# The lag-kernel matmuls of a state space layer, given by steps over four column positions

## The chip, the cores and the metric

The kernel runs on one core of a Trainium2 chip. The metric is the device time of one execution in microseconds (us), lower is better. TensorE is called PE here, VectorE DVE, ScalarE ACT, GpSimd POOL, and SyncE, whose queue starts most transfers, SP.

## The reference, cut to what matters

Two layers of a hybrid backbone over 512 latent tokens and 256 context tokens of 1024 channels. Each layer has three mixers (spatial gating, a bidirectional diagonal state space, pooling), an output projection and a SwiGLU feed-forward. The change touches the state space alone, of which the reference computes, for each of 32 groups of 16 channels with 64 states and in two directions:

```python
def diag_scan(lam_bar, bu, h0, reverse):
    ...
    _, h = lax.associative_scan(combine, (a, bu), reverse=reverse, axis=1)
    return h

    for k, reverse in enumerate((False, True)):
        lam_bar, b_bar = ssm_discretize(lam_re[k], lam_im[k], log_dt[k], b_re[k], b_im[k])
        cm = lax.complex(c_re[k].astype(jnp.float32), c_im[k].astype(jnp.float32))
        ...
        h_lat = diag_scan(lam_bar, bu_lat, h_end, reverse)
        y_lat = y_lat + jnp.einsum('ghp,blgp->blgh', cm, h_lat).real
```

The kernel computes this in chunks of 8 tokens. Inside a chunk, what a token gives to one at a distance of m tokens is a 16 x 16 matrix per group, the real part of C lam^m B, for m from -7 to 7. These matrices are the lag kernels.

## The kernel before, in words

Products of float32 with float32 are made from split operands (`mm3`, lines 144 to 146: three matmuls of a high and a low part). The small ones of the state space's tables are float32 matmuls by `mm` (line 149), each of which appears in the trace as two records. The accumulators in PSUM are tiles named acc, aux, pr and md; pr and md have one buffer each.

`ssm_prep` makes a layer's tables, block by block. In layer 0 a block has 8 groups (4 blocks, before the mixers, while the input projection runs); the powers X, XF and Y of B and C lie in one buffer named pz. In layer 1 a block has 4 groups (8 blocks, made beside the feed-forward of layer 0); X, XF and Y have tiles of their own names. bb holds B, Cc holds C. A block goes through: the turn tables (Tt), the powers X by DVE and ACT, a reversed copy XF, their transposes on PE (line 599) for the table E, the powers Y (line 543 in layer 0), and the lag kernels.

The lag kernels (lines 627 to 646) are made in two halves, each into a tile pr. A matmul handles two groups: its weights are 32 columns of bb, and its output lies on 32 partitions of pr, the column position j (0 to 3 in layer 0, 0 and 1 in layer 1; the `tile_position` 0, 32j). For each j and each of the real and imaginary parts i, the first half has one matmul with Cc (128 rows by 32 columns of the array, 32 columns of data) and one with Y (64 rows by 32 columns, 224 columns of data). The second half has one matmul for each j and i, with XF (64 rows by 32 columns, 224 columns of data, at row 64). ACT (line 648) and DVE (line 649) then take the result into klag, and POOL's queue stores it as Kd, from where the mixer loads it as T.

The kernel is written for a framework whose scheduler sets each engine's order from its own estimate of the times. Where a change alters those, the order of other work near it moves as well. The fillers of layer 1's tables and the modulation vectors (tiles wm from w_mod, bm and md) are issued between the steps of the feed-forward and of the mixers.

Of the kernel before, what the change touches and what calls it, by code (L numbers as in the profile page):

```python
# [86 lines left out]
def tile_backbone(ctx, tc, A, out):  # L87
# [65 lines left out]

    # ------------------------------------------------------------- constants
    ident = cst.tile([128, 128], F32, name="ident")
# [34 lines left out]

    # ------------------------------------------------------------ modulation
    def first_mod_loads():
        """w_mod for the first shift and scale, by blocks of 256 channels: [block][shift, scale][chunk]."""
        big_ = bigt([128, 3, 8, 256], F32, "wmod")
        where = {(0, 0): "rawm", (0, 1): "raw", (1, 0): "whi", (1, 1): "wlo", (2, 0): 0, (2, 1): 1, (3, 0): 2,
                 (3, 1): "rawm"}
        res = {}
        for (j, m), w in where.items():
            c_ = slice(1024 * m + 256 * j, 1024 * m + 256 * j + 256)
            if isinstance(w, int):  # L200
                t = big_[:, w]
                dma(t, A["w_mod"][0, :, c_].rearrange("(t p) c -> p t c", p=128))
                res[j, m] = [t[:, k] for k in range(8)]
            else:
                res[j, m] = []
                for h in range(2):
                    t = wp.tile([128, 4, 256], F32, tag=w, name=nm("wm"), bufs=2)
                    dma(t, A["w_mod"][0, 512 * h:512 * h + 512, c_].rearrange("(t p) c -> p t c", p=128))
                    res[j, m] += [t[:, k] for k in range(4)]
        return res  # L210
# [48 lines left out]
    def mod_rows_v(l, m, res, lanes):  # L259
        """The same rows with the products summed over the chunks on the vector engine."""  # L260
        accs = [q4([128, 1024], s="macc") for _ in range(lanes)]
        for k in range(8):
            raw = wp.tile([128, 1024], F32, name=nm("wm"), tag="rawm", bufs=2)
            dma(raw, A["w_mod"][l, k * 128:(k + 1) * 128, m * 1024:(m + 1) * 1024])
            for r in range(lanes):
                c_ = csil[:, 2 * k + r:2 * k + r + 1]
                if k == 0:
                    V.tensor_scalar(accs[r], raw, c_, None, op0=ALU.mult)
                else:
                    V.scalar_tensor_tensor(accs[r], raw, c_, accs[r], op0=ALU.mult, op1=ALU.add)  # L270
            yield
        bm = wp.tile([1, 1024], F32, name=nm("bm"), tag="rawm", bufs=2)
        dma(bm, A["b_mod"][l:l + 1, m * 1024:(m + 1) * 1024])
        ps = mdt()
        for j in range(4):
            c_ = slice(256 * j, 256 * j + 256)
            mm(ps[32 * j:32 * j + 32, :256], bc(ident[0:1, 0:1], [1, 32]), bm[:, c_], start=True, stop=False,
               tile_position=(0, 32 * j))
        for r in range(lanes):
            for j in range(4):  # L280
                mm(ps[32 * j:32 * j + 32, :256], osel[:, 31 - r:63 - r], accs[r][:, 256 * j:256 * j + 256],
                   start=False, stop=r == lanes - 1, tile_position=(0, 32 * j))
        M = sp.tile([128, 256], F32, tag="M", name=nm("M"), bufs=1)
        S.copy(M, ps[:, :256])
        res.append(M)
# [44 lines left out]

    # ------------------------------------------------------------ norm -> hT
    def sumsq(x, junk):
# [4 lines left out]
    def norm_tile(x, dg, junk):  # L337
        """The RMS factors of a tile's tokens, as a diagonal that the transpose multiplies by."""
        ss = sumsq(x, junk)
        r = rsq(ss, 1, 1.0 / D)  # L340
        S.activation(dg, ident, AF.Copy, scale=r[:, 0:1])
# [32 lines left out]

    # ------------------------------------------------------------ SSM tables
    ssm = {}

    def ssm_params():
# [10 lines left out]
        def expo(x, t, h, sc):  # L389
            # exp(x) - 1 = sc * h + (sc - 1), sc a power of two; x is overwritten, h becomes sc * h  # L390
            V.tensor_scalar(t, x, 1.0 / math.log(2.0), MAGIC_EXP, op0=ALU.mult, op1=ALU.add)
# [56 lines left out]
        V.tensor_mul(qi, t, inv)  # L448
        # transposed, [(k,p), quantity, l, g]: lam, turn, q with pairs (-im, im), and the decay
        PT = cst.tile([128, 8, 2, G], F32, name="PT")  # L450
# [34 lines left out]
    def cmul(o, a_, b_, t):  # L485
        """o = a * b for pairs (re, im) [128, 2, groups, n]; b per group, (re, (-im, im))."""
        shape = list(o.shape)
# [11 lines left out]
    def prep_load(l):  # L499
        """B and C of a layer: B with (k, state) on the partitions, C with (group, channel)."""  # L500
        Br, Cr = q4([128, 2, 512], s="Br"), q4([128, 2, 4, 2, 64], s="Cr")
# [7 lines left out]
    def ssm_prep(l, Br, Cr, bufs=None):  # L509
        """The layer's tables for the chunks, block by block of 8 groups; the two directions lie on  # L510
        the partitions, (direction, state); C and its powers are kept conjugated."""
        lam, lamc = ssm["lam"], ssm["lamc"]
# [22 lines left out]
        def last_step(T, p):  # L535
            """T[4:8] = T[0:4] * p for every group, the products by the real part on the scalar engine."""
            for g in range(ng):
# [18 lines left out]
        for g0 in range(0, G, ng):  # L556
# [71 lines left out]
            for half in range(2):  # L628
                ps = prt()
                n = (128, 112)[half]  # L630
                pv = ps[:, :2 * n].rearrange("p (g c) -> p g c", g=2)
                for j in range(ng // 2):
                    jr = slice(32 * j, 32 * j + 32)
                    g2 = slice(2 * j, 2 * j + 2)
                    for i in range(2):
                        c0 = 16 * g0 + 32 * j
                        lh = bb[:, i, c0:c0 + 32]
                        if half == 0:
                            mm(pv[jr, :, 0:16], lh, Cb[:, i, g2, :], start=i == 0, stop=False,
                               tile_position=(0, 32 * j))  # L640
                            mm(pv[jr, :, 16:128], lh[0:64],
                               Y[0:64, i, g2, 0:7, :].rearrange("p g m h -> p g (m h)"),
                               start=False, stop=i == 1, tile_position=(0, 32 * j))
                        else:
                            mm(pv[jr], lh[64:128], XF[64:128, i, g2, 1:8, :].rearrange("p g m h -> p g (m h)"),
                               start=i == 0, stop=i == 1, tile_position=(64, 32 * j))
                o = slice(112, 240) if half == 0 else slice(0, 112)
# [8 lines left out]

    # ------------------------------------------------------------ the mixers
    def load_small(l):
# [53 lines left out]
    def mix_C_lat(l, pz, i, pbd, mac, poolL):  # L712
        """Tiles i and i + 1, whose z share a bank."""
        q = f4([128, 1024], "cmix")
# [29 lines left out]
    def ssm_UV(l, bt, U, vt, ET=None):  # L744
        """The chunks' inputs to the states, the backward direction's in its own order."""
        Et, tab = ET or load_ET(l, bt, q4([128, 1024], s="E"), q4([128, 768], s="tab"))
# [22 lines left out]
    def ssm_rot(l, bt, vt, tab, wk):  # L769
        """The states at the chunks' starts: turn, scan, turn back."""  # L770
        T1, T2, T3, S_, dec = wk
# [26 lines left out]
    def ssm_y(l, bt, U, FT, S_, yst, g_):  # L798
        """The outputs of a block's groups, moved to (group, channel) on the partitions, tokens (t, c)."""
        Ft, T_ = FT  # L800
# [26 lines left out]
    def mixing(l, hhi, hlo, small, filler):  # L827
# [133 lines left out]
        next(op)  # L961
        # gate of the SSM output
        mb = bigt([128, 2, 4, 768], F32R, "mb")
# [30 lines left out]
    def square(src, ss, h):  # L994
        """The sum of squares of a column half, into its column of ss."""
        jk = f4([128, 512], "jk")
        S.activation(jk, src, AF.Square, accum_out=ss[:, h:h + 1])  # L997

    def residual(xt, u, ss):
        """xt += rms factor * u, u being the products of G and m, ss the sums of m's squares."""  # L1000
        r = rsq(ss[:, 0:1], 1, 1.0 / D, more=ss[:, 1:2])
        V.scalar_tensor_tensor(xt, u, r[:, 0:1], xt, op0=ALU.mult, op1=ALU.add)
# [5 lines left out]
    def out_proj(l, mac, Gs):  # L1008
        """A first step with the products that need only the A and C parts, then the rest."""
        lat_only = l == DEPTH - 1  # L1010
# [181 lines left out]

    # =============================================================== program
    xall = bigt([128, 6, 1024], F32, "xall")
# [136 lines left out]
```

## Time and profile before

| | us |
|---|---|
| median of 3 runs | 1600.65 (1595.11 to 1605.75) |
| span of the profiled execution | 1596.2 |
| PE busy | 1524.7 |
| DVE busy | 858.9 |
| ACT busy | 631.9 |
| POOL busy | 143.4 |

The profile is of one execution. Times in the rows are us from the start of its span. PE is TensorE's matmuls and PEld its weight loads; a busy time of PE includes the modelled end of a matmul, so records overlap and start times tell more than durations. PEclk is the granted clock of TensorE, 1.00 at full speed (2.4 GHz).

### The profile page before, as it was taken

What the parts mean: (1) busy time and instruction counts of PE and PEld (TensorE: products, weight loads), DVE (VectorE), ACT (ScalarE), POOL (GpSimd) and SP (SyncE); (2) the same over time, 40 slices, a digit from 0 to 9 for tenths busy, and PEclk for the clock granted to TensorE, in tenths of its full rate; (3) what the DMA queues carried; (4) which work ended last, traced back from release to release, by engine and by line L of the source; (5) the groups of instructions that cost most, each with busy time, mean ns of one, the idle gap of its engine ahead of it and who ended that gap; (6) DMA issues with size and microseconds to landing.
All of it is one profiled execution on the core that took longest, in us unless ns stands there. A gap on an engine that the chain in (4) does not pass through costs nothing.

```text
span 1596.2 us, 22394 instructions
## 1 busy us (share of the span) xinstructions
PE 1524.7 (96%) x8649; PEld 1243.1 (78%) x8649; DVE 858.9 (54%) x1549; ACT 631.9 (40%) x1184; POOL 143.4 (9%) x244
## 2 busy tenths in 40 slices
PE   4999999998999999999999999899898999999996
PEld 2576787787888877888878888798777888888885
DVE  7476797446464675545564334768566332333335
ACT  3466755536332233333221223655456223222222
POOL 2111220003000000000000000322002000000001
PEclk9999999999999999999999999999999999999998
DMA  9468798675133455234466322657565333332332
GB/s 290 171 188 284 254 289 276 199 221 179 53 116 99 137 181 172 91 104 122 157 201 219 93 73 85 213 169 231 149 205 191 100 106 93 94 105 93 94 104 79
DMA packets 227435, 250.71 MB, mean 157 GB/s; under 512 B 50040, under 2 KB 172132, under 8 KB 226816
## 3 DMA queue, kind: packets, MB, share of 16 engines
q1 hardware_dynamic: 217364, 214.26, 43.3%
q0 software_dynamic: 9088, 34.58, 6.1%
q8 instruction: 68, 1.11, 0.3%
q10 hardware_dynamic: 876, 0.44, 0.1%
q14 instruction: 39, 0.32, 0.1%
HBM read 206.80 MB, written 42.43 MB: 156 GB/s over the span
## 4 chain that ended last, share of the span: by engine, by line
PE 83%; DMA 7%; ACT 3%; DVE 3%; POOL 2%; SPq 1%; issue 1%; DVEq 0%; POOLq 0%; ACTq 0%
PE acc L144 20%; PE acc L146 19%; PE acc L145 19%; PE pr L149 5%; PE aux L144 4%; PE aux L146 4%; PE aux L145 4%; PE md L149 4%; PE aux L149 2%; DMA wm<-in_w_mod_dram 2%; ACT w L133 1%; DMA yd<-zslot 1%; DVE w L134 1%; POOL rs L187 1%; DMA tab<-Td 1%
## 5 line engine op out<-in xcount | busy, mean ns | idle before, releaser
L144 PE MATMUL acc<-h,w 128*128 128x512 f32 (+1 forms) x1248 | 431.1, 348 | 5.1 <-DVE h L370 2.8
L145 PE MATMUL acc<-h,w 128*128 128x512 f32 (+1 forms) x1248 | 432.1, 347 | 3.2 <-DVE h L371 3.1
L146 PE MATMUL acc<-h,w 128*128 128x512 f32 (+1 forms) x1248 | 430.3, 346 | 1.4 <-DVE w L134 1.4
L134 DVE TENSOR_TENSOR w<-raw,w 128x1024 fp32r<-128x1024 f32 x190 | 232.3, 1223 | 340.5 <-ACT w L133 327.8
L133 ACT CAST w<-raw 128x1024 fp32r<-128x1024 f32 x190 | 199.3, 1049 | 407.2 <-PE acc L145 228.9
L144 PEld LDWEIGHTS acc<-h,w 128*128 128x128 f32 x1248 | 236.9, 191 | 37.8 <-DVE h L370 3.4
L145 PEld LDWEIGHTS acc<-h,w 128*128 128x128 f32 x1248 | 237.9, 191 | 34.3 <-DVE h L371 4.3
L146 PEld LDWEIGHTS acc<-h,w 128*128 128x128 f32 x1248 | 237.8, 191 | 32.1 <-issue 2.2
L1113 DVE TENSOR_TENSOR fsg<-fsg,acc 128x512 f32<-128x512 f32 (+1 forms) x68 | 39.8, 585 | 158.7 <-PE acc L146 157.3
L145 PE MATMUL aux<-w,act 128*128 128x512 f32 x220 | 86.3, 392 | 0.0
L146 PE MATMUL aux<-w,act 128*128 128x512 f32 x220 | 86.2, 392 | 0.0
L145 PE MATMUL acc<-w,act 128*128 128x512 f32 x220 | 86.0, 391 | 0.0
L146 PE MATMUL acc<-w,act 128*128 128x512 f32 x220 | 86.0, 391 | 0.0
L144 PE MATMUL acc<-w,act 128*128 128x512 f32 x220 | 83.1, 392 | 0.0
L144 PE MATMUL aux<-w,act 128*128 128x512 f32 x220 | 83.0, 391 | 0.0
L270 DVE SCALAR_TENSOR_TENSOR macc<-wm,csil,macc 128x1024 f32<-128x1024 f32 x56 | 70.6, 1277 | 5.7 <-DMA wm<-in_w_mod_dram 5.6
L1114 ACT CAST act<-fsg 128x512 fp32r<-128x512 f32 (+1 forms) x68 | 36.5, 537 | 91.3 <-DVE fsg L1113 91.3
L1112 ACT ACTIVATE fsg<-acc 128x512 f32<-128x512 f32 (+1 forms) x68 | 34.8, 511 | 83.5 <-PE acc L146 83.5
L145 PE MATMUL acc<-w,h 128*128 128x512 f32 (+1 forms) x160 | 55.6, 348 | 0.8 <-DVE w L134 0.8
L146 PE MATMUL acc<-w,h 128*128 128x512 f32 (+1 forms) x160 | 55.4, 346 | 0.0
L185 POOL TENSOR_TENSOR rs<-ss 128x1 f32<-128x1 f32 x20 | 7.6, 381 | 526.2 <-ACT jk L997 525.3
L144 PE MATMUL acc<-w,h 128*128 128x512 f32 (+1 forms) x160 | 54.6, 353 | 0.0
(364 smaller groups left out, 2395.1 us busy)
## 6 DMA issues: line engine op xcount, KB each, us to landing
wm<-in_w_mod_dram SPq DMA_DIRECT2D x90, 512.0 KB
raw<-in_ffn_w_gate_dram SPq DMA_DIRECT2D x44, 512.0 KB
raw<-in_ffn_w_up_dram SPq DMA_DIRECT2D x44, 512.0 KB
raw<-in_ffn_w_down_dram SPq DMA_DIRECT2D x44, 512.0 KB
raw<-in_w_in_dram SPq DMA_DIRECT2D x28, 512.0 KB
raw<-in_w_out_dram SPq DMA_DIRECT2D x26, 512.0 KB
xt<-xd SPq DMA_DIRECT2D x18, 512.0 KB
Ed<-Et POOLq DMA_DIRECT2D x16, 512.0 KB, 4.6
```

The lines of the kernel that those rows point to most:

```text
L133: S.copy(hi, raw)
L134: last_v[0] = V.tensor_sub(lo, raw, hi)
L144: PE.matmul(ps, lhi, rhi, start=start, stop=False, skip_group_check=True)
L145: PE.matmul(ps, lhi, rlo, start=False, stop=False, skip_group_check=True)
L146: return PE.matmul(ps, llo, rhi, start=False, stop=stop, skip_group_check=True)
L149: return PE.matmul(ps, lhsT, rhs, start=start, stop=stop, skip_group_check=True, **k)
L185: GP.tensor_tensor(t[:, :n], ss, more, op=ALU.add)
L187: GP.tensor_scalar(t[:, :n], ss, scale, EPS, op0=ALU.mult, op1=ALU.add)
L270: V.scalar_tensor_tensor(accs[r], raw, c_, accs[r], op0=ALU.mult, op1=ALU.add)
L1112: S.activation(sg[:, :n], p1[:, :n], AF.Silu)
L1113: V.tensor_mul(sg[:, :n], sg[:, :n], p2[:, :n])
L1114: S.copy(act[0][:, fl, o:o + n], sg[:, :n])
```

## The change

The loops over position and part in the first and second half are replaced by a list of jobs, each with the number of its step, which is sorted by that number. The matmuls and their operands stay the same. In the first half the steps are Cc real, Y real, Cc imaginary, Y imaginary, each over all positions; in the second half XF real, XF imaginary. Comments and docstrings are removed as well, which changes line numbers by up to 2.

```diff
-                for j in range(ng // 2):
-                    jr = slice(32 * j, 32 * j + 32)
-                    g2 = slice(2 * j, 2 * j + 2)
-                    for i in range(2):
+                jobs = []
+                for i in range(2):
+                    for j in range(ng // 2):
                         c0 = 16 * g0 + 32 * j
-                        lh = bb[:, i, c0:c0 + 32]
+                        lh, jr, g2 = bb[:, i, c0:c0 + 32], slice(32 * j, 32 * j + 32), slice(2 * j, 2 * j + 2)
                         if half == 0:
-                            mm(pv[jr, :, 0:16], lh, Cb[:, i, g2, :], start=i == 0, stop=False,
-                               tile_position=(0, 32 * j))
-                            mm(pv[jr, :, 16:128], lh[0:64],
-                               Y[0:64, i, g2, 0:7, :].rearrange("p g m h -> p g (m h)"),
-                               start=False, stop=i == 1, tile_position=(0, 32 * j))
+                            jobs.append((2 * i, pv[jr, :, 0:16], lh, Cb[:, i, g2, :], i == 0, False, (0, 32 * j)))
+                            jobs.append((2 * i + 1, pv[jr, :, 16:128], lh[0:64],
+                                         Y[0:64, i, g2, 0:7, :].rearrange("p g m h -> p g (m h)"),
+                                         False, i == 1, (0, 32 * j)))
                         else:
...
+                jobs.sort(key=lambda job: job[0])
+                for _, o_, l_, r_, st, en, tp in jobs:
+                    mm(o_, l_, r_, start=st, stop=en, tile_position=tp)
```

The order on PE in layer 1, third block, first half, as the difference of the change against before (the operand Cc or Y names the step, the last numbers are the output's shape, x2 is two matmuls in a row):

```order
-L149 MATMUL pr_5225<-Y_5155,bb_4031 32x2x112
-L149 MATMUL pr_5225<-Cc_4032,bb_4031 32x2x16
-L149 MATMUL pr_5225<-Y_5155,bb_4031 32x2x112
-L149 MATMUL pr_5225<-Cc_4032,bb_4031 32x2x16
-L149 MATMUL pr_5225<-Y_5155,bb_4031 32x2x112
-L149 MATMUL pr_5225<-Cc_4032,bb_4031 32x2x16
-L149 MATMUL pr_5225<-Y_5155,bb_4031 32x2x112
+L149 MATMUL pr_5225<-Y_5155,bb_4031 32x2x112 x2
+L149 MATMUL pr_5225<-Cc_4032,bb_4031 32x2x16 x2
+L149 MATMUL pr_5225<-Y_5155,bb_4031 32x2x112 x2
```

The same seven matmuls, now six with one of them moved ahead, stand in the same place; the first step, Cc of both positions (before: of the first), stands some rows ahead. The other blocks of layer 1 read alike.

The order on PE in layer 0, first block, first half, of the change (pz is the buffer of Y; acc is the input projection, md the modulation, from the bias bm and the weights wm):

```order
L144 MATMUL acc_937<-h_470,w_907 128x512
L149 MATMUL pr_713<-pz_344,bb_346 32x2x112
L145 MATMUL acc_937<-h_471,w_907 128x512
L146 MATMUL acc_937<-h_470,w_908 128x512
L149 MATMUL md_973<-bm_974,ident 32x256
L149 MATMUL pr_713<-pz_344,bb_346 32x2x112
L149 MATMUL md_973<-bm_974,ident 32x256 x3
L149 MATMUL pr_713<-pz_344,bb_346 32x2x112
L149 MATMUL md_973<-wm_980,csil 32x256
L149 MATMUL pr_713<-pz_344,bb_346 32x2x112
L149 MATMUL pr_713<-Cc_347,bb_346 32x2x16 x4
L149 MATMUL pr_713<-pz_344,bb_346 32x2x112 x4
```

Before, pz and Cc alternate here without a break, eight and seven times, and bm and wm follow as x4 each. Now the first Y step lies in four pieces between them; the Cc step before it stands far ahead. In the second and third block the first Y step lies in three pieces (of 1, 2 and 1 matmuls).

The order on PE in layer 0, fourth block, first half, first of before (up to the first interruption by acc):

```order
L149 MATMUL aux_1692<-zslot_904 128x96 x4
L149 MATMUL pr_1651<-pz_344,bb_346 32x2x112
L149 MATMUL pr_1651<-Cc_347,bb_346 32x2x16
L149 MATMUL pr_1651<-pz_344,bb_346 32x2x112
L149 MATMUL pr_1651<-Cc_347,bb_346 32x2x16
L149 MATMUL pr_1651<-pz_344,bb_346 32x2x112
L149 MATMUL pr_1651<-Cc_347,bb_346 32x2x16
L144 MATMUL acc_1974<-w_1979,h_470 128x512
```

and of the change:

```order
L149 MATMUL aux_1692<-zslot_904 128x96 x4
L149 MATMUL pr_1651<-pz_344,bb_346 32x2x112 x4
L149 MATMUL pr_1651<-Cc_347,bb_346 32x2x16 x4
L149 MATMUL pr_1651<-pz_344,bb_346 32x2x112 x4
L144 MATMUL acc_1974<-w_2003,h_470 128x512
```

Here all steps are whole, and the projection's matmuls that stood between them now stand ahead. SP's order has the same transfers; between about the start of layer 0's tables and the end of its mixers, loads of w_mod, w_in, E, F and T have changed places with each other. From layer 1's mixers on, the orders of all engines are equal.

## Rows read from the trace of the kernel before

**Rows 1.** The page's head.

```profile
span 1596.2 us, 22394 instructions
```

**Rows 2.** Stretches: start:end, length, busy us (instructions) by engine, clock, DMA share, GB/s.

```profile
85.00:200.00 115.00, 115.00 (x750) 78.17 (x749) 81.66 (x243) 78.06 (x173) 21.65 (x37) 0.96 0.75 239
...
98.10:104.80 6.70, 6.70 (x37) 4.29 (x37) 5.28 (x20) 4.19 (x11) 0.00 (x0) 0.55 0.59 185
152.80:156.10 3.30, 3.30 (x10) 2.68 (x10) 1.83 (x5) 0.37 (x1) 0.00 (x0) 0.61 1.03 337
200.00:310.00 110.00, 100.15 (x815) 80.91 (x815) 73.81 (x126) 59.10 (x131) 13.51 (x13) 0.97 0.84 267
490.00:860.00 370.00, 370.00 (x2056) 293.89 (x2055) 210.83 (x348) 112.49 (x195) 22.49 (x40) 1.00 0.48 153
```

**Rows 3.** PE in time order, layer 0, block 1, first half: start, us, instruction.

```profile
92.48 0.56 PE L149 MATMUL pr<-pz,bb 64*32 64x224 f32 x2
92.97 0.25 PE L149 MATMUL pr<-Cc,bb 128*32 128x32 f32 x2
93.15 0.56 PE L149 MATMUL pr<-pz,bb 64*32 64x224 f32 x2
...
97.18 0.83 PE L149 MATMUL pr<-pz,bb 64*32 64x224 f32 x2
97.94 0.80 PE L145 MATMUL acc<-h,w 128*128 128x512 f32 x1
```

**Rows 4.** PE in time order, layer 0, block 1, second half.

```profile
104.47 0.28 PE L146 MATMUL acc<-h,w 128*128 128x256 f32 x1
104.59 0.28 PE L144 MATMUL acc<-h,w 128*128 128x256 f32 x1
104.80 0.98 PE L149 MATMUL pr<-pz,bb 64*32 64x224 f32 x16
105.71 0.38 PE L145 MATMUL acc<-h,w 128*128 128x256 f32 x1
```

**Rows 5.** The same, only what has started by 104.95 us.

```profile
104.80 0.41 PE L149 MATMUL pr<-pz,bb 64*32 64x224 f32 x4
```

**Rows 6.** PE in time order, layer 1, block 1, first half.

```profile
495.92 0.56 PE L149 MATMUL pr<-Y,bb 64*32 64x224 f32 x2
496.41 0.25 PE L149 MATMUL pr<-Cc,bb 128*32 128x32 f32 x2
496.59 0.56 PE L149 MATMUL pr<-Y,bb 64*32 64x224 f32 x2
...
498.42 0.50 PE L145 MATMUL acc<-h,w 128*128 128x512 f32 x1
```

**Rows 7.** PE in time order, layer 1, block 1, second half.

```profile
502.90 0.95 PE L149 MATMUL pr<-XF,bb 64*32 64x224 f32 x8
503.78 0.39 PE L144 MATMUL acc<-h,w 128*128 128x256 f32 x1
```

**Rows 8.** The chain that ended last, layer 0's tables: start, us, what, records.

```profile
92.55 5.46 PE pr L149 x30
...
113.91 0.57 PE md L149 x8
...
122.95 0.42 PE md L149 x3
...
124.68 0.47 PE md L149 x4
...
147.93 4.95 PE pr L149 x28
```

**Rows 9.** ACT's waits, 85 to 200 us: total us, times, longest.

```profile
ACT klag L648 <- PE pr L149: 17.4, 6, 5.4
```

**Rows 10.** The chain that ended last, layer 0's mixers.

```profile
202.78 7.93 DMA raw<-in_w_out_dram
...
212.03 6.31 DMA E<-Ed
```

More of the change, by code (lines that the diff above doesn't have):

```diff
@@ L631, in ssm_prep @@
                 pv = ps[:, :2 * n].rearrange("p (g c) -> p g c", g=2)
-                for j in range(ng // 2):
-                    jr = slice(32 * j, 32 * j + 32)
-                    g2 = slice(2 * j, 2 * j + 2)
-                    for i in range(2):
+                jobs = []
+                for i in range(2):
+                    for j in range(ng // 2):
                         c0 = 16 * g0 + 32 * j
-                        lh = bb[:, i, c0:c0 + 32]
+                        lh, jr, g2 = bb[:, i, c0:c0 + 32], slice(32 * j, 32 * j + 32), slice(2 * j, 2 * j + 2)
                         if half == 0:
-                            mm(pv[jr, :, 0:16], lh, Cb[:, i, g2, :], start=i == 0, stop=False,
-                               tile_position=(0, 32 * j))
-                            mm(pv[jr, :, 16:128], lh[0:64],
-                               Y[0:64, i, g2, 0:7, :].rearrange("p g m h -> p g (m h)"),
-                               start=False, stop=i == 1, tile_position=(0, 32 * j))
-                        else:
-                            mm(pv[jr], lh[64:128], XF[64:128, i, g2, 1:8, :].rearrange("p g m h -> p g (m h)"),
-                               start=i == 0, stop=i == 1, tile_position=(64, 32 * j))
+                            jobs.append((2 * i, pv[jr, :, 0:16], lh, Cb[:, i, g2, :], i == 0, False, (0, 32 * j)))
+                            jobs.append((2 * i + 1, pv[jr, :, 16:128], lh[0:64],
+                                         Y[0:64, i, g2, 0:7, :].rearrange("p g m h -> p g (m h)"),
+                                         False, i == 1, (0, 32 * j)))
+                        else:
+                            jobs.append((i, pv[jr], lh[64:128],
+                                         XF[64:128, i, g2, 1:8, :].rearrange("p g m h -> p g (m h)"),
+                                         i == 0, i == 1, (64, 32 * j)))
+                jobs.sort(key=lambda job: job[0])
+                for _, o_, l_, r_, st, en, tp in jobs:
+                    mm(o_, l_, r_, start=st, stop=en, tile_position=tp)
                 o = slice(112, 240) if half == 0 else slice(0, 112)
```

## The prediction

> **What bounds the kernel now.** I read the page's first part, then the windows by stretch, then TensorE's instructions in time order where the lag kernels stand, then who waits for them. The span is 1596.2 us [rows 1]; the three runs have a median of 1600.65 us, so 4.5 us (0.3%) are added to a span to compare it with runs. In the stretch in which layer 1's tables are made, 490 to 860 us, PE is busy 370.00 of 370.00 us, DVE 211 and ACT 112, and the clock is 1.00 [rows 2]: whatever PE saves there shortens the kernel, because the feed-forward matmuls stand right behind it in the same queue. In the stretch of layer 0's tables, 85 to 200 us, PE is also busy 115.00 of 115.00 us [rows 2], but DVE (82) and ACT (78) are close, and the work is chained: ACT alone stood idle 17.4 us for the lag kernels' results, once for 5.4 us [rows 9]. From 200 to 310 us PE is busy 100 of 110 us and the DMA engines 0.84 of the time [rows 2]; there the chain of work that ended last goes through loads of 6 to 8 us [rows 10].
>
> **What the lag kernels cost now.** A block has two halves. The first half multiplies on two sizes of tile: Cc, 128 rows by 32 columns, and Y (in layer 0 its name is pz, the buffer it lives in), 64 rows by 32 columns. Each float32 matmul shows as two records, so "x2" is one matmul. In layer 0 the sequence is pz, Cc, pz, Cc: starts at 92.48, 92.97, 93.15 and so on to 97.18 and the next acc at 97.94 [rows 3]. A pair takes (97.18 - 92.48) / 7 = 0.671 us, of which 0.49 from a pz to the next Cc and 0.18 from a Cc to the next pz. Layer 1 has the same steps: 495.92, 496.41, 496.59 [rows 6]. Nothing of one position runs beside another here.
>
> The second half has one size of tile only, and the code before gives it position by position too. Yet its 16 records (four positions, four records each) take 105.71 - 104.80 = 0.91 us [rows 4], four of them have started by 104.95 [rows 5], and with two positions in layer 1 the 8 records take 503.78 - 502.90 = 0.88 us [rows 7]. So four positions already run side by side there, and two more positions cost 0.03 us. I conclude two things. The second halves gain nothing from the new order. And what keeps the first half serial is the change of tile size between Cc and Y, which now comes at every matmul.
>
> The Trainium skill, "TensorE: Matmul & The Clock Gate", Part 3, section "The mechanism", speaks against this: matmuls start and end strictly in program order, and a weight load runs beside a matmul in flight only where the row group differs, and the four column positions share theirs. By that rule the second half of before would be serial, and the new order would overlap nothing (0 us gained); by rows 4, 5 and 7 it is not serial, and the measurement decides.
>
> **The change, step by step.** It adds and removes no matmul and no DMA: 4 x (16 + 8) in layer 0 and 8 x (8 + 4) in layer 1 make 192 before and after. With equal steps together, a first half has four stages: Cc, Y, Cc, Y. A stage is priced by the single matmul plus what further positions cost in the second halves (0.01 to 0.02 us each): with four positions Y 0.49 + 0.04 = 0.53 and Cc 0.18 + 0.04 = 0.22; with two, 0.505 and 0.195.
>
> Layer 1, eight blocks of two positions. Before, the first Cc stands alone earlier and then seven matmuls stand together: 498.42 - 495.92 = 2.50 us [rows 6]. After, the order has Y x2, Cc x2, Y x2 together: 0.505 + 0.195 + 0.505 = 1.205. Gain 1.30 us a block, 10.4 us for eight. PE has no idle time there, so I count all of it. The bounds: 0 if the positions do not overlap, 10.4 if they do as in the second halves.
>
> Layer 0, four blocks of four positions. Before, 8 Y and 7 Cc: 8 x 0.49 + 7 x 0.18 = 5.18 us a block; the chain of waits has 5.46 us with its start for the first one [rows 8]. After, the scheduler does not leave all stages whole, as the order shows. Block 1: the first Y stage is four single matmuls with others between, then Cc x4, Y x4: 4 x 0.49 + 0.22 + 0.53 = 2.71, with one more change of tile from a 128 x 128 matmul (104.80 - 104.59 = 0.21 against 0.12 between its equals, about 0.1 [rows 4]), and md is split twice. An md group of 8 records takes 0.57 us whole and 0.42 + 0.47 in two parts [rows 8], 0.32 more each time. So 2.71 + 0.1 + 0.64 = 3.45, gain 1.7. Blocks 2 and 3: the first Y stage is in three pieces, 0.49 + 0.505 + 0.49, plus 0.22 + 0.53 and two entries of 0.1 = 2.4; gain 2.8, and for block 2 another 0.3 because its own md group is whole again, 3.1. Block 4 has its stages whole: 0.53 + 0.22 + 0.53 = 1.28, gain 3.9. Sum 1.7 + 3.1 + 2.8 + 3.9 = 11.5 us of PE's time.
>
> How much of the 11.5 reaches the end? For it: PE never idles in the stretch, and ACT's 17.4 us of idle time before klag [rows 9] shrink with it. Against it: in each block DVE and ACT do the next table in series behind klag, and 71% and 68% busy leaves them little room; and at 200 us the kernel enters the stretch that loads bound. SP's loads of w_mod, E and T are moved against each other there, none is added; they wait for buffers that PE and DVE free, and start earlier if those do. The bounds are 0 and 11.5; nearer to the upper, because PE is what all wait for; I take three quarters, 8.6 us.
>
> The clock. The granted clock was full until the first block's 5.5 us of small matmuls and then 0.55 on average from 98.1 to 104.8 us; after the third block's 5 us the same, 0.61 from 152.8 to 156.1 [rows 2, 3, 8]. So the lower level, 1.2 of 2.4 GHz, came twice right behind such a run. At full clock these stretches would be shorter by up to 6.7 x 0.45 = 3.0 and 3.3 x 0.39 = 1.3 us. Block 1's run stays long after the change (singles between md matmuls, which are small as well), block 3's becomes about 1.3 us before acc follows. I count the second, 1.3, and leave the first as it is; bounds 0 and 4.3.
>
> Sum: 10.4 + 8.6 + 1.3 = 20.3 us. The span becomes 1596.2 - 20.3 = 1575.9, the time 1600.65 - 20.3 = 1580 us.
>
> **The rivals.** (A) The forecast, 1580 us.
>
> (B) Layer 0's part is swallowed: the DVE and ACT chain, or the loads of 200 to 310 us, end when they did. Only layer 1 gains: 1600.65 - 10.4 = 1590 us. For it: the 0.84 DMA share and the loads on the chain [rows 2, 10]. Against: DMA share is 0.75 before that stretch, so the engines could start earlier.
>
> (C) All passes through and the clock stays up: 10.4 + 11.5 + 4.3 = 26.2, 1574 us.
>
> (D) The change does not do what it says: positions with equal tiles do not overlap in the first half, a Y still takes 0.49 us and a Cc 0.18. Then nothing is gained and the time is the old one, 1600 us. For it: no two matmuls of a first half overlap now [rows 3, 6]. Against: the second halves do [rows 4, 5, 7]. The rule of the Trainium skill quoted above ("TensorE: Matmul & The Clock Gate", Part 3) would give this case.
>
> (E) Slower. The scheduler's new order in 200 to 310 us puts a load that PE needs behind loads of w_mod in SP's queue, as with E, 6.3 us, and w_out, 7.9 us [rows 10]. Each such new wait costs 6 to 8 us; about three cancel the forecast gain, and it takes (20 + 16) / 6.3, about six, to be over 1% slower: 1617 us. Against: the order of SP has the same loads in nearly the same places, and from layer 1's mixers on PE's order is the old one.
>
> **How the numbers follow.** A 0.57, B 0.24, C 0.11, D 0.04, E 0.04. The range 1570 to 1592 takes in A, B and C, each with some microseconds for the scatter of the runs; D and E, 0.08, and some scatter are left out. Over 1% is 16 us, about what a measurement of this kernel can tell from no change. Below 1584.6 lie C and most of A (0.49), so faster 0.60; within 1% the rest of A, B and D, 0.36; slower 0.04.
>
> **What would show it.** In the changed profile: in layer 1 three stages of two matmuls in about 1.2 us in place of 2.50, and two records of Y starting within 0.02 us of each other (if they start 0.2 us or more apart, D). In layer 0, block 4's 12 matmuls in about 1.3 us; block 1's still 3 us or more. The second halves unchanged at 0.88 and 0.91. The stretch from the first layer-1 block to the last shorter by some 10 us. ACT's idle time before klag well under 17 us. If the mixers' stretch ends at the old time although PE reached it earlier, B. The clock at about 153 us tells the last term. The weakest step is the three quarters for layer 0.

## The result, and the profile after

The changed kernel takes 1580.48 us (median of 4 runs, 1574.39 to 1582.81). Beside it the kernel before took 1597.88 us (4 runs, 1593.86 to 1605.75). The ratio is 0.9864, with a 95% interval of 0.9832 to 0.9896 (the quotient of the two medians alone, 0.9891, lies in it): it is faster by over 1%. The forecast was 1580 us, faster. Executions of one kernel differ by some microseconds with the mean granted clock: of the change, 1574.39 us at 0.986 and 1582.07 at 0.981. The profiled execution took 1578.89 us; a span of 1575.9 us was forecast.

The page's head, which answers to [rows 1]:

```profile
span 1577.1 us, 22403 instructions
```

Stretches of the changed kernel, columns as in [rows 2]. The first two are the places where the forecast looked for the clock:

```profile
94.60:101.40 6.80, 6.80 (x43) 4.52 (x43) 6.42 (x26) 1.46 (x5) 0.00 (x0) 0.52 0.98 292
142.00:156.00 14.00, 14.00 (x106) 9.64 (x105) 12.14 (x35) 11.13 (x24) 2.21 (x5) 1.00 0.96 293
490.00:860.00 370.00, 370.00 (x2113) 300.14 (x2112) 214.13 (x351) 114.30 (x197) 21.77 (x38) 1.00 0.48 153
```

Between 490 and 860 us PE starts 57 more matmul records than before and is never idle, as before. Some of these are work that has moved into the window; the landmarks below compare equal work.

Layer 1, block 1, PE in time order, first half and second half (answers to [rows 6] and [rows 7]):

```profile
485.32 0.57 PE L149 MATMUL pr<-Y,bb 64*32 64x224 f32 x4
485.81 0.26 PE L149 MATMUL pr<-Cc,bb 128*32 128x32 f32 x4
486.00 0.57 PE L149 MATMUL pr<-Y,bb 64*32 64x224 f32 x4
486.50 0.50 PE L144 MATMUL acc<-h,w 128*128 128x512 f32 x1
...
491.07 0.95 PE L149 MATMUL pr<-XF,bb 64*32 64x224 f32 x8
491.95 0.39 PE L146 MATMUL acc<-h,w 128*128 128x256 f32 x1
```

The three stages (six matmuls; a Cc stands ahead with its stage) take 486.50 - 485.32 = 1.18 us where seven matmuls took 2.50. A Y stage of two positions takes 0.49 us, as one matmul did before. The second half takes 0.88 us, as before.

Layer 0 of the changed kernel, PE in time order: the beginning and the end of block 1's first half, then block 4's first half, then block 4's second half (answers to [rows 3] and [rows 4]):

```profile
90.57 0.56 PE L149 MATMUL pr<-pz,bb 64*32 64x224 f32 x2
...
95.31 0.33 PE L149 MATMUL pr<-Cc,bb 128*32 128x32 f32 x8
95.57 0.97 PE L149 MATMUL pr<-pz,bb 64*32 64x224 f32 x8
96.47 1.07 PE L149 MATMUL md<-wm,csil 128*32 128x256 f32 x6
...
167.30 0.58 PE L149 MATMUL pr<-pz,bb 64*32 64x224 f32 x8
167.81 0.27 PE L149 MATMUL pr<-Cc,bb 128*32 128x32 f32 x8
168.01 0.58 PE L149 MATMUL pr<-pz,bb 64*32 64x224 f32 x8
168.53 0.96 PE L144 MATMUL acc<-w,h 128*128 128x512 f32 x3
...
176.91 0.96 PE L149 MATMUL pr<-pz,bb 64*32 64x224 f32 x16
177.80 2.02 PE L149 MATMUL aux<-zslot,E 128*128 128x96 f32 x16
```

Block 4 shows the change at its clearest: four positions take 0.51 us for a Y stage (8 records) and 0.20 us for a Cc stage, 1.23 us for the three. In block 1 the clock has already fallen: its last Y stage takes 0.90 us. Counted from the start of each group of records to the start of PE's next instruction, the first halves of layer 0's four blocks take 22.0 us in the kernel before and 9.9 in the change.

ACT's waits from 85 to 200 us (answers to [rows 9]; total us, times, longest):

```profile
ACT klag L650 <- PE pr L149: 4.3, 3, 2.3
```

**Where the lead arises and where it goes.** Three landmarks on PE divide the span: the first matmul with E in layer 0's mixers (aux<-zslot,E), the first product with gT at these mixers' end, and the first and last Y of layer 1. Of the kernel before, from the views by tile (durations in ns, then first and last start in us):

```profile
L149 PE MATMUL aux<-zslot,E x224: 243/275/497, 194.2 to 1127.9; 128*128 128x96 f32 x112
L144 PE MATMUL aux<-gT,w x64: 277/334/469, 301.9 to 1176.4; 128*128 128x384 f32 x32, 128*128 128x256 f32 x32
L149 PE MATMUL pr<-Y,bb x64: 349/361/373, 495.9 to 839.9; 64*32 64x224 f32 x64
```

The same three of the changed kernel:

```profile
L149 PE MATMUL aux<-zslot,E x224: 243/275/350, 177.8 to 1106.9; 128*128 128x96 f32 x112
L144 PE MATMUL aux<-gT,w x64: 277/334/469, 292.2 to 1157.0; 128*128 128x384 f32 x32, 128*128 128x256 f32 x32
L149 PE MATMUL pr<-Y,bb x64: 349/361/373, 485.3 to 817.9; 64*32 64x224 f32 x64
```

The lead is 194.2 - 177.8 = 16.4 us at the first E, with 999 matmul records ahead of it in both kernels. It is 9.7 at gT, 10.6 at the first Y and 22.0 at the last Y; the end has 1596.2 - 1577.1 = 19.1. So layer 0's tables give 16.4 us, its mixers take 6.7 back, 0.9 comes before the first Y, layer 1's tables give 839.9 - 495.9 - (817.9 - 485.3) = 344.0 - 332.6 = 11.4 us, and 2.9 go after the last Y. These 2.9 can't be put down to the change: from the last Y to the end the kernel before takes 756.3 us here, the change 759.2, and e2 below, with PE's order of before throughout, 1595.6 - 836.1 = 759.5.

### The profile page after: what moved, and what is told of

The parts are those of the page before. It is cut to its first block, busy times and chain, and to the rows that moved or that the text cites. A ratio compares the mean times of both kernels' runs of the same rounds, so it can differ in the third digit from the quotient of the medians.

```text
span 1577.1 us, 22403 instructions
## 1 busy us (share of the span) xinstructions
PE 1501.6 (95%) x8649; PEld 1231.8 (78%) x8649; DVE 859.6 (55%) x1549; ACT 632.8 (40%) x1184; POOL 143.3 (9%) x244
## 4 chain that ended last, share of the span: by engine, by line
PE 82%; DMA 5%; ACT 4%; DVE 4%; POOL 2%; SPq 1%; issue 1%; DVEq 0%; POOLq 0%; ACTq 0%
PE acc L144 20%; PE acc L145 19%; PE acc L146 19%; PE aux L146 4%; PE aux L144 4%; PE aux L145 4%; PE md L149 4%; PE pr L149 3%; PE aux L149 3%; DMA wm<-in_w_mod_dram 2%; ACT w L133 1%; DVE w L134 1%; DVE xt L1004 1%; POOL rs L187 1%; POOL rs L188 1%
```

## The experiments

Theory S: what was dear before is the change of tile size between Cc and Y at every matmul; matmuls of one size on different column positions overlap whatever their order. Its rivals: that the order of the positions itself matters (P), and, for layer 0, that something other than PE's own time decides what reaches the end. All edits but f3's and the h pair's are on the sort of the list of jobs, so that the matmuls stay the same. Between kernels of different runs the ratio to the kernel before in the same runs is compared.

| kernel | order of the first half | us (lowest to highest, runs) | ratio to before |
|---|---|---|---|
| the change | by steps | 1580.48 (1574.39 to 1582.81, 4) | 0.9864 [0.9832, 0.9896] |
| e2 | by position; second half by steps | 1598.16 (1595.90 to 1600.79, 10) | 0.9988 [0.9969, 1.0007] |
| e3 | by steps in layer 1 alone | 1590.39 (1587.76 to 1591.85, 6) | 0.9938 [0.9913, 0.9963] |
| e4 | by steps in layer 0 alone | 1588.86 (1586.72 to 1591.47, 6) | 0.9930 [0.9904, 0.9956] |
| f3 | as before, Cc on 64 rows | 1582.75 (1576.65 to 1587.63, 4) | 0.9879 [0.9837, 0.9920] |
| f1 | two sizes, each by position | 1578.19 (1577.44 to 1584.82, 6) | 0.9873 [0.9850, 0.9896] |
| j2 | f1 once more | 1581.80 (1574.24 to 1582.03, 5) | 0.9863 [0.9838, 0.9888] |
| f2 | two sizes, each by steps | 1586.52 (1581.97 to 1590.16, 6) | 0.9914 [0.9890, 0.9937] |
| j1 | layer 0 by steps, layer 1 two sizes | 1575.77 (1574.65 to 1580.08, 5) | 0.9833 [0.9810, 0.9856] |
| h1 | by steps, half of w_mod's loads | 1579.30 (1577.45 to 1580.57, 4) | 0.9873 [0.9844, 0.9901] |
| h2 | as before, half of w_mod's loads | 1602.69 (1596.94 to 1607.85, 10) | 1.0004 [0.9985, 1.0023] |

### e2: the second half alone

```diff
-                jobs.sort(key=lambda job: job[0])
+                jobs.sort(key=lambda job: job[6][1] if half == 0 else job[0])
```

(`job[6][1]` is the column position; the first half is as before.)

> Only the second half of the lag kernels is given by steps; the first half stays position by position, and every engine's order is that of the kernel before. Theory S (what costs is the change of tile size between Cc and Y; the order of the positions does not matter): no change, 1598 us within 3, a second half still at 0.91 us (layer 0) and 0.88 us (layer 1). Rival P (positions overlap only when given one after the other): the second halves get shorter, by up to 0.4 us each, 12 of them, so 1593 us.

Measured: ratio 0.9988, its interval reaches over 1. Nothing is gained that can be told. The second half's eight matmuls of one size (sixteen records) take 0.89 us by steps in layer 0 (99.24 to 100.13 us in e2) and 0.91 by position [rows 4], and 0.88 either way in layer 1, so the order of positions by itself is not what the change gains by.

### f3: one tile size, the order of before

```diff
-                            mm(pv[jr, :, 0:16], lh, Cb[:, i, g2, :], start=i == 0, stop=False,
+                            mm(pv[jr, :, 0:16], lh[0:64], Cb[0:64, i, g2, :], start=i == 0, stop=False,
```

> The kernel before, its order on every engine kept (position by position), but the matmul with Cc uses 64 rows of the array in place of 128, so that all matmuls of a first half have one size of tile. It leaves out the backward direction's share at lag 0. Theory S: the positions overlap although they are given one by one; a first half takes about 1.0 us in place of 5.2 (layer 0) and about 0.95 in place of 2.5 (layer 1); PE is spared 4 x 4.2 + 8 x 1.5 = 29 us, of which the loads of the mixers' stretch swallow some 6: about 1575 us. Rival P: 0.67 us a pair as before, 1598 us.

Layer 0, block 1, first half of f3, PE in time order:

```profile
89.97 0.56 PE L149 MATMUL pr<-pz,bb 64*32 64x224 f32 x2
90.37 0.25 PE L149 MATMUL pr<-Cc,bb 64*32 64x32 f32 x4
90.43 0.57 PE L149 MATMUL pr<-pz,bb 64*32 64x224 f32 x4
...
90.91 0.57 PE L149 MATMUL pr<-pz,bb 64*32 64x224 f32 x4
...
92.32 0.50 PE L145 MATMUL acc<-h,w 128*128 128x512 f32 x1
```

With the order of before and without a change of size, the whole first half takes 92.32 - 89.97 = 2.35 us instead of 5.46. This shows the cause: the size, not the order, made the first half serial. The total, 0.9879, is as good as the change's within the intervals, and 8 us above the 1575 us expected. For 2.35 us is more than twice what was expected, and layer 1's 1.40 us (485.67 to 487.07, before 2.50) stands against 0.95. The records come as x4, which reads as one matmul of each of two neighbouring positions, at 0.48 us a position: only two overlap. In the second half, where a position has only four records, the sixteen of all four take 0.91 us; here a position has eight, of Cc and Y in turn. No run varied the count by itself, so what limits the overlap stays open.

### e3 and e4: one layer at a time

```diff
-                jobs.sort(key=lambda job: job[0])
+                jobs.sort(key=lambda job: job[0] if l == 1 else job[6][1])
```

(e3; e4 has `l == 0`.)

> The new order in layer 1 only; layer 0 has the order of before on every engine. By the prediction's sum 8 x 1.30 = 10.4 us, all of it at the end: 1587.5 us within 3. If the feed-forward were not bound by PE there, less: 1593 us or more.

> The new order in layer 0 only; layer 1 has the order of before. The prediction counted 8.6 us and 1.3 for the clock; the trace of the change shows the input projection's end 9 us earlier than before at 300 us, after a lead of 16 to 20 us at 180 to 245 us. If the swallowing by loads is real: 1588 to 1590 us. If the lead came through in full (11.5 us and more): 1583 us or less.

The first and last Y of e3, then of e4, by tile:

```profile
L149 PE MATMUL pr<-Y,bb x64: 349/361/373, 495.2 to 827.8; 64*32 64x224 f32 x64
```

```profile
L149 PE MATMUL pr<-Y,bb x64: 349/361/373, 485.7 to 829.7; 64*32 64x224 f32 x64
```

By the medians, e3 is 1600.75 - 1590.39 = 10.4 us faster than before in the same runs (6 to 14 by its interval), and 2.9 us above the 1587.5 expected, inside its 3. From its first to its last Y it takes 332.6 us, exactly as the change does, against 344.0. e4 is 1600.75 - 1588.86 = 11.9 us faster (7 to 15), within the 1588 to 1590 us expected if the mixers take part of it back, and its Y stretch takes 344.0 us, exactly as before. The two add up to 22.3 us; the change's own gain by its interval is 17 to 27 us (1.04% to 1.68% of 1600). Layer 1's term stands as forecast, and layer 0's can't be told from the 9.9 us (8.6 + 1.3) counted for it.

### f1 and f2: only two stages, by position and by steps

```diff
-                jobs.sort(key=lambda job: job[0])
+                jobs.sort(key=lambda job: (job[0] % 2, job[6][1]) if half == 0 else job[0])
```

(f1: all Cc, then all Y, each position by position; f2 has `job[0]` in place of `job[6][1]` and goes by steps.)

> The same two runs of one tile size, but within each position by position (four records of a position, then four of the next). Theory S, as the run with Cc on 64 rows refined it (matmuls of one tile size overlap across positions when a position has no more than four records ahead of the others): the same time as by steps, within 2 us, and four records of four positions starting within 0.05 us. Rival P (only matmuls given one after the other on different positions overlap): the Y of a block of layer 0 takes 8 x 0.4 = 3.2 us in place of 0.95, of layer 1 1.7 in place of 0.9, so 4 x 2.3 + 8 x 0.8 = 15 us more: 1592 us.

> The first half in two runs of one tile size: all matmuls with Cc (real, then imaginary), then all with Y, each by steps. One change of tile size in place of three. Both theories: in layer 1 the four matmuls with Y take 0.9 us together, where the change takes 1.18 for Y, Cc, Y: 8 x 0.28 = 2.2 us less than the change; in layer 0 some 0.35 us a block less, partly swallowed. 1577 to 1579 us against 1580.5 of the change.

The Y matmuls of layer 1's block 1 in f1, then in f2:

```profile
482.97 0.95 PE L149 MATMUL pr<-Y,bb 64*32 64x224 f32 x8
483.85 0.50 PE L144 MATMUL acc<-h,w 128*128 128x512 f32 x1
```

```profile
497.91 0.95 PE L149 MATMUL pr<-Y,bb 64*32 64x224 f32 x8
498.79 0.50 PE L144 MATMUL acc<-h,w 128*128 128x512 f32 x1
```

Both take 0.88 us for all eight records, by position or by steps, in place of the change's 1.18 us for its three stages. That decides between S and P: once a size stands together, the order inside it makes no difference here.

As totals the two differ: f2 missed its expectation by some 8 us, and f1's, that the two agree within 2 us, fails with it. The difference does not lie in layer 1 (both take 327.7 us from the first Y to the last) but in layer 0, where the scheduler made two different orders of the work around the tables. f2 reaches the first E at 184.9 us and gT only at 304.6, later than before (301.9); f1 takes 184.3 to 289.5. In that stretch f2's PE is idle 119.7 - 104.0 = 15.7 us, at a clock of 0.93, and f1's 105.2 - 96.5 = 8.7 us, at 0.95. The two traces are f2's slowest execution and f1's fastest and show more than the 8 us between the medians; how much of these is the order and how much the clock was not taken apart. The price of the lag kernels in layer 1 came out as counted. f1's gain over before came out again in j2:

> The same kernel as f1, once more beside j1: 1578.2 us was its median against 1601.8 of the kernel before. If its gain over the change (1580.5) is real, it comes out again at a ratio of 0.987 or below to the kernel before; at 0.988 or above the two can't be told apart.

Its ratio, 0.9863, is below the 0.987 named there, but so is the change's own, 0.9864: f1 can't be told from the change.

### j1: two stages in layer 1 alone

```diff
-                jobs.sort(key=lambda job: job[0])
+                jobs.sort(key=lambda job: (job[0] % 2, job[0]) if half == 0 and l == 1 else (0, job[0]))
```

> The change, with the first half of layer 1 alone in two sizes only: all Cc matmuls first, then all Y (layer 0 stays as the change has it). In layer 1 the stages Cc, Y, Cc, Y become Cc, Y, so one change of tile size back and forth goes: the 8 records of Y take 0.95 us at once in f2, against 1.18 us for the last three stages in the change, 0.23 us a block, 1.8 us for eight. Theory S (the change of tile size is the price): 1580.5 - 1.8 = 1578.7 us, 1576 to 1582, not to be told from the change by its time alone; from the first layer-1 Y to the last, 2 us shorter than in the change. Rival O (the order near the tables, which the scheduler moves in layer 1 as well, matters more than the tables' own time): the lead of f2 over the change in layer 1, 12.7 against 10.9 us, was chance, and the time differs from 1578.7 by over 4 us either way.

The first and last Y of j1:

```profile
L149 PE MATMUL pr<-Y,bb x64: 349/349/373, 484.3 to 811.9; 64*32 64x224 f32 x64
```

1575.77 us is the lowest median of all, just under the range expected. But its interval (0.9810 to 0.9856) overlaps the change's, and its five executions had a mean granted clock of 0.987, the change's four 0.984; the change's two at 0.986 and 0.987 took 1574.39 and 1578.89 us. That j1 is faster than the change is not shown. The Y stretch takes 327.6 us, 5.0 less than in the change, where 2 were expected. A block's Cc and Y cost 0.25 + 0.87 us in place of 0.18 + 1.18, so 0.24 x 8 = 1.9 us are the matmuls, as counted. Another 2.3 us lie in one place, between block 7's second half and block 8's first (25.29 us in place of 27.57, with 134 records in place of 146): the scheduler has put other work elsewhere. Most of that looks moved and not gained: at the last Y j1's trace is 6.0 us ahead of the change's, at the end 1577.1 - 1574.0 = 3.1.

### h1 and h2: half of w_mod's loads

Layer 0's mixers give back 6.7 of the 16.4 us. There PE waits most for the modulation's weights wm, so the first suspect was their loads. In both kernels the loads are halved, h1 from the change and h2 from the kernel before, and half of these weights is left out:

```diff
-            dma(raw, A["w_mod"][l, k * 128:(k + 1) * 128, m * 1024:(m + 1) * 1024])
+            dma(raw[:, 0:512], A["w_mod"][l, k * 128:(k + 1) * 128, m * 1024:m * 1024 + 512])
...
-                mm(ps[32 * j:32 * j + 32, :256], csil[:, 2 * k:2 * k + 32], raw[:, 256 * j:256 * j + 256],
+                mm(ps[32 * j:32 * j + 32, :256], csil[:, 2 * k:2 * k + 32], raw[:, 256 * (j % 2):256 * (j % 2) + 256],
```

> The changed kernel, but the loads of w_mod beside layer 0's mixers bring half the columns, and the matmuls use those twice; it leaves out half of those weights. To be compared with the same edit of the kernel before. If these loads swallow what layer 0 gains: this one has the same lead over its partner at 180 us (16 us) and at 290 us, and ends 26 us ahead of it. If they do not: 10 us at 290 us as between the change and before, and 18 us at the end.

> The kernel before with the same half loads of w_mod; the partner of the run above. If the mixers' stretch of the kernel before is bound by these loads too, it is faster than before by some 10 us (four loads of 4 to 6 us on the chain become half as long): 1590 us. If not, 1600 us.

h2 is no faster than before (1.0004), and h1 no faster than the change (0.9873 against 0.9864): half the loads do not shorten either kernel. h1's trace reaches the first E 15.5 us ahead of h2's (179.8 and 195.3) and gT 10.8 us ahead (292.1 and 302.9), and ends 22.2 us ahead, between the 26 and the 18 that were named. So 4.7 us are given back with half the loads as well. The stretch from the first E to gT in h1, then in h2, columns as in [rows 2]:

```profile
179.80:292.10 112.30, 104.05 (x837) 81.65 (x837) 75.59 (x130) 61.83 (x142) 15.97 (x17) 0.94 0.73 227
195.30:302.90 107.60, 97.02 (x825) 77.01 (x822) 72.81 (x126) 58.93 (x139) 15.74 (x16) 0.97 0.72 218
```

PE is idle 112.30 - 104.05 = 8.3 us in h1 and 10.6 in h2, so with half the loads what is given back is busy time alone, 7.0 us more, at a lower clock and with 12 more records. So the loss does not go away with half of w_mod's loads, but its idle part does, and that these loads take no part of the lead is not shown. Nor is the pair a clean one, because the scheduler gave PE another order up to gT in both kernels.

### What takes the lead in layer 0's mixers

The stretch from the first E to gT, in one window each, columns as in [rows 2]: the kernel before, the change, j1, f3.

```profile
194.20:301.90 107.70, 97.85 (x816) 79.47 (x815) 74.48 (x127) 59.90 (x139) 13.51 (x13) 0.97 0.81 257
```

```profile
177.80:292.20 114.40, 101.26 (x810) 80.96 (x807) 79.45 (x134) 62.54 (x143) 15.59 (x15) 0.94 0.81 258
```

```profile
178.90:290.80 111.90, 98.27 (x811) 78.96 (x808) 79.24 (x134) 62.67 (x143) 17.60 (x15) 0.97 0.82 261
```

```profile
178.50:291.80 113.30, 102.61 (x816) 82.90 (x815) 74.43 (x127) 60.02 (x140) 12.19 (x13) 0.92 0.79 247
```

In the change the stretch is 6.7 us longer, in two parts. PE is busy 3.4 us more for slightly fewer records, at a clock of 0.94 against 0.97. And PE is idle 114.40 - 101.26 = 13.1 us against 9.9. j1 and e4 have the same order of PE's matmuls as the change up to gT. e4 has the 114.4 us at 0.94 once more; j1 has a clock of 0.97 in this execution, and its stretch is 2.5 us shorter. Against the kernel before, at the same clock, j1 is still 4.2 us longer, nearly all of it idle time (13.6 us against 9.9). So the clock is worth some 2.5 to 3.4 of the 6.7 us, and the waits are the rest. In f3, with the clock at 0.92, nearly all of the 5.6 us is busy time (4.8). PE's waits in these windows of the kernel before and of the change:

```profile
PE md L149 <- DMA wm<-in_w_mod_dram: 6.4, 6, 1.7
PE aux L149 <- DMA E<-Ed: 1.7, 1, 1.7
PE pr L149 <- DVE wk L777: 0.9, 1, 0.9
PE pr L149 <- DMA pc<-in_k_pc_dram: 0.5, 1, 0.5
```

```profile
PE md L149 <- DMA wm<-in_w_mod_dram: 7.4, 8, 1.9
PE aux L149 <- ACT wk L798: 2.2, 1, 2.2
PE pr L149 <- DMA pc<-in_k_pc_dram: 1.7, 1, 1.7
PE acc L144 <- ACT mac L710: 0.8, 1, 0.8
```

No single wait has grown by the missing 3.3 us: wk (2.2 for ACT, where before 0.9 for DVE), pc (1.2 more), wm (1.0 more) and mac (0.8) share it, and E's wait shrinks by 1.3. PE arrives earlier, and several inputs are then a little late in turn; which of them is first to blame was not taken apart.

## Why the prediction was right, point by point

**What makes the first half serial** was the change of tile size: f3 shows it with the order of before, and e2, f1 and f2 show that the order alone is worth nothing. The Trainium skill, "TensorE: Matmul & The Clock Gate", Part 3, section "The mechanism", lets matmuls end in program order and weight loads overlap only across row groups; here the four positions share their row group, and eight records of Y on four positions take 0.51 us where two on one took 0.49. The measurement decides, and rival D falls. (That this rule makes the four positions serial was the prediction's own step.) The Trainium skill, "TensorEngine Tiling (Array Packing)", section "Key Properties", says that changing the tiling mode drains TensorE; the trace agrees in kind, and this case has the price of taking turns: a Y and a Cc in turn cost 0.671 us a pair, of which stages of four positions leave (0.51 + 0.20) / 4 = 0.18.

**Layer 1, 10.4 us.** Forecast block 1.205 us, measured 1.18, so 8 x 1.32 = 10.6; e3's medians give 10.4 us by themselves, and the Y stretch of every kernel with layer 1 by steps (the change, e3, h1) is 332.6 us in place of 343.9 to 344.0. All of it passes, because PE stays busy 370.00 of 370.00 us, as the prediction read from [rows 2].

**Layer 0, 11.5 us of PE's time, 8.6 passing, and the clock's 1.3.** Block 4 was forecast as 1.28 us and took 1.23, and the four first halves together became 12.1 us cheaper (22.0 - 9.9). Up to the first E the lead is 16.4 us, more than 11.5 + 1.3. Some 1.9 of this stood there ahead of block 1 already (its first Y starts at 90.57 us, before at 92.48 [rows 3]), by a low stretch of the clock before the tables that this execution doesn't have. Before and after:

```profile
39.60:46.40 6.80, 6.80 (x23) 3.77 (x22) 5.61 (x19) 5.96 (x16) 1.30 (x2) 0.52 1.11 369
```

```profile
39.60:46.40 6.80, 6.80 (x49) 4.51 (x50) 5.67 (x16) 6.80 (x19) 1.31 (x2) 1.00 1.10 373
```

The change does not touch this place, so these 1.9 us are no part of its gain. That leaves 14.5 us against 12.8: about the forecast, somewhat low. Then 6.7 are given back before gT. What passes, which the prediction called its weakest step, is 9.7 - 1.9 = 7.8 us by this one pair of traces; e2 and e3, with layer 0 as before, reach gT at 299.4 and 301.2 us, 7.2 and 9.0 after the change. By e4's runs it is 7 to 15 us. The 9.9 counted lies among these, with some luck: the tables gave more than was counted, and half of it passed rather than three quarters, a share that the prediction took without a row for it. The reason given for the loss holds in part: the prediction looked to DVE, ACT and loads of 200 to 310 us, which fits the idle part, but 2.5 to 3.4 us of the loss are a clock that falls there more than before.

**The clock.** In this trace the first low stretch stayed (94.6 to 101.4 us, 0.52, the level of 1.2 GHz), from within block 1's first half on; the second, behind block 3, went (142 to 156 us, 1.00). Both as forecast, but the other runs do not bear out the reason, a long run of small matmuls. e2 has PE's order of before throughout, and its clock is full around block 1, whose first half takes 5.2 us, and low around block 3:

```profile
90.00:107.00 17.00, 17.00 (x116) 10.54 (x116) 13.34 (x37) 7.58 (x17) 2.40 (x8) 1.00 0.73 205
143.00:160.00 17.00, 17.00 (x87) 10.56 (x87) 10.53 (x32) 8.87 (x22) 1.09 (x2) 0.80 0.69 216
```

e3, with the same order up to gT, has it the other way round (0.70 and 1.00 in these windows). Of the eight traces with a cheaper first half in layer 0, four have a low stretch at block 1 (the change, e4, j1, f1) and none has one from 143 to 160 us; of the four with that of before, two have the first (before, e3) and three the second (before, e2, h2). So the 1.3 us are likely the change's, and that the 3.0 us stayed was this execution's chance. Not forecast were the low stretches in layer 0's mixers, 13.7 us in all. The longest of them:

```profile
258.40:265.20 6.80, 6.80 (x40) 5.13 (x34) 3.04 (x5) 0.96 (x2) 0.00 (x0) 0.52 0.61 199
```

The kernel before has 6.8 us there (217.6 to 224.4 us, 0.56). f3, whose block 1 is 2.35 us long, has no low stretch at blocks 1 and 3, but loses as much later (0.92 in the mixers above), so that rival C's 4.3 us did not reach the end there either.

**ACT's wait for klag** fell from 17.4 to 4.3 us, as forecast. **Rival B**, all of layer 0's part swallowed, falls with e4. **Rival E**, slower by a load that comes late, came true in small: 1.2 us more for pc and 1.0 for wm, not 6 to 8. f2 shows how much another order of layer 0's work can go with, since its gT comes later than before; by its trace no wait there is longer than 2.9 us, and part of its loss is the clock.

## What to carry to other kernels

Put small matmuls of one tile size together before you think of their order over the column positions: here the change of size kept the positions from overlapping, and it was paid at every change (0.671 us a pair, 0.18 in stages). Price such a gain stage by stage from a place in the trace where one size already stands together, and count it in full only where TensorE has no idle time; elsewhere follow the lead from landmark to landmark, since waits or a lower clock can take part of it back (6.7 of 16.4 us here). Compare a stretch in several traces with the same order before you give a microsecond or two of it a cause. Where a scheduler sets the order, a change of the list moves other work as well, and the total with it (f2 against f1 and j2: 5 to 8 us with the same lag kernels in two stages).

## What the runs showed of the hardware

- Matmuls of one tile size on different column positions overlapped, whether given by position or by steps: at full clock the sixteen records of a second half took 0.89 to 0.91 us in every kernel (1.09 in e3's block 1, in a low stretch).
- With eight records to a position and one tile size, only two neighbouring positions overlapped (f3: 2.35 us for four). What limits it stays open.
- A Cc of 128 rows that alternates with a Y of 64 rows costs 0.671 us a pair; with Cc cut to 64 rows, 0.48 us a position for two pairs.
- The granted clock fell to 0.52 or so, with PE busy all the time, at places that differ between executions with the same order of PE's matmuls (e2 and e3 in layer 0's tables; 0.94 in the change and 0.97 in j1 in its mixers); a difference of 2 to 3 us in one stretch can be the clock alone.
